# The Mixer's tenth load buffer, the order of sums in the first FFN sets, and the bank order of the up products

## The chip, the cores and the metric

The kernel runs on one core of a Trainium2 chip. The metric is device time in microseconds (us), the median of several runs; a profile is one execution taken by the hardware profiler. TensorE (PE in the profile) multiplies, VectorE (DVE) and ScalarE (ACT) work elementwise, GpSimd (POOL) and SyncE (SP) mostly issue transfers here. PEld is TensorE's weight load.

## The reference

One block of a network on 512 tokens of width 1024, in float32:

```python
x = x + 0.5 * swiglu(rmsnorm(x, g1), ffn1_w_gu, ffn1_w_down)      # D_FF = 2816
x = x + hybrid_mixer(rmsnorm(x, gm), w_in, ...)                   # convolution + gated linear attention
x = x + 0.5 * swiglu(rmsnorm(x, g2), ffn2_w_gu, ffn2_w_down)
out = rmsnorm(x, final_g)

def swiglu(x, w_gu, w_down):
    g, u = split(x @ w_gu, 2)
    return (silu(g) * u) @ w_down
```

`hybrid_mixer` multiplies x by `w_in` into conv inputs, q, k, v, a low-rank gate (`g_lr`, 16 columns), r and two output gates, and ends in `w_out_conv`, `w_out_gla` and `w_o`.

## The kernel before

**Products.** Each float32 product is made of three TensorE products of a high and a low part: `W.take()` gives a weight tile as `wh` (a ScalarE cast, L427) and `wl` (the rest, a VectorE subtraction, L430). Large products are done in *sets* by Strassen's scheme with seven products, named m1, p2, q6, p5, q7, p4, p3, each on sums of blocks of the weight and of the operand. The remaining columns are *plain units*: in each FFN one group of two up pairs (`mm_group`, four weight units of two k blocks each, over the eight k blocks of the width), and in the Mixer eight units for q and k (a group for heads 0 and 1 in four units, then four single columns) and eight of `w_out_conv`.

**The planner.** `PLAN` lists the weight blocks in order and `STEPS` the steps that use them, one unit or one of the seven products each. `Weights.issue` does one step: it starts loads ahead of time (`fetch`, `load_set`), makes sums of weight blocks (on VectorE at L404, or by an accumulating transfer on POOL at L390), and casts. It runs two steps ahead of the products. `Weights.slot(until)` picks the buffer for a load or sum: there are nine buffers of their own (`f0` to `f8`), and in the Mixer a tenth, which is a tile of the pool `op`. Each carries in `until` the last step that uses it; the one with the least value is taken. The tenth begins at -1. The pool `op` has 15 tiles and holds above all the high and low parts of the operands.

**The order of work.** The Tile framework plans each engine's queue when the program is built, from its own estimates of durations, mostly in the order in which the program is written among what it takes to be ready. `tc.issue_after(i)` holds the instructions of a block that run on the engine of `i` behind `i` in that engine's queue. `W.after_row`, `W.behind` and `W.lead` hand such an instruction to the next weight sum, the next cast and the next `wl`.

**Between FFN1 and the Mixer.** FFN1's down product ends in p4. Inside it, blocks of the result are transposed back (`back(i)`: L1281 on TensorE, L1285 on VectorE) and added to x, and `nxt.add(i)` makes the Mixer's operand for k block i (L541 on ScalarE, L542 on VectorE, squares at L552 and L553). The sum of p4's own result is L1222. `turned_out` and `turned_in` (L1183, L1189) turn other blocks by way of memory, on SyncE's queue; `grown` (L1272) adds them to x. The Mixer begins with `gl_raw`, a small load on SyncE (L1431) of the gate's 16 columns, which VectorE spreads into `gl_w` (L1437 to L1441). Its first group of products (L504) has `gate_k(k)` behind each k block: the transposes of block 4 + k for the first four, then two products of the gate (L1459, L1460) into an `aux` bank.

**An FFN's up sets.** The group gives the sums of two plain pairs in four banks; `plain_pair` multiplies the gate sums by the row of the norm (L1097) and applies Silu, and the result is multiplied into `hid[0]` later. Then ten sets run, each over two columns of g and u, in the order m1, p2, p5, q6, (next m1), q7, (next p2), p4, p3 for the first. `PairSet` keeps three pairs of PSUM banks for a set: a in `x`, b and c rotating over `w`, `z`, `y`; set 0 has b in `w` and c in `y`. `onto` adds a bank pair to a tile (two additions on L823), `whole` copies one half out (ScalarE, L830) and adds the other (VectorE, L831), `taken` makes the value of q6 or q7 (L813 to L815). p3 accumulates in c, so it can't start before the sum with c on q7 has been read. `banks("pairs", tags)` lays out the four tags in the order of the letters, two banks each.

**An FFN's down sets.** Two sets of 10 and 12 k blocks; `bank_of(new)` gives a set its banks: a the pair `A`, b two from `new`, c two more of the pool `mm`. The pool `mm` has six banks and `aux` two.

Of the kernel before, what the change touches and what calls it, by code (L numbers as in the profile page):

```python
# [11 lines left out]
AF = mybir.ActivationFunctionType  # L12
ALU = mybir.AluOpType
# [117 lines left out]
SLOTS = 9  # L131
# [62 lines left out]
def block_kernel(ctx: ExitStack, tc: tile.TileContext, xT, vecs, gf, gup, wgl, wts, out):  # L194
# [104 lines left out]
    class Weights:  # L299
# [3 lines left out]
        def __init__(self, ahead):  # L303
            self.ahead = ahead
            self.issued = 0
            self.taken = 0
            self.end = 0
            self.ready = []
            self.raw = {}
            self.loads = {}  # L310
            self.more = {}
            self.sums = {}
            self.first = {}
            self.until = [-1] * (SLOTS + 1)
            self.slots = SLOTS
            self.behind = None
            self.after_row = None
            self.lead = None
            self.added = None

# [30 lines left out]

        def slot(self, until):

            i = min(range(self.slots), key=lambda j: self.until[j])
            self.until[i] = until
            if i == SLOTS:
                return tile_of("op", [P, 1024])
            cnt[0] += 1
            return pools["f"].tile([P, 1024], F32, tag=f"f{i}", name=f"f{cnt[0]}")
# [33 lines left out]
        def issue(self):  # L393
            at = self.issued
            self.fetch(at)
            for n in self.loads.get(at, ()):
                self.load_set(n)
            for n in self.sums.get(at, ()):
                a11, _, a21, a22, _ = self.raw[n]
                w = unit_cols(PLAN[n])  # L400
                if not lean(n):
                    s3 = self.raw[n][4] = self.slot(STEPS.index((n, "q7")))
                    with ExitStack() if self.after_row is None else tc.issue_after(self.after_row):
                        self.summed = nc.vector.tensor_tensor(out=s3, in0=a11, in1=a21,  # L404
                                                              op=ALU.add).ins
                    self.after_row = None
                self.first[n] = (self.add(a21[:, :w], self.block(n + 3), self.added) if lean(n)
                                 else self.add(a21, a22))
            for n, i in self.more.get(at, ()):
                a = STEPS.index((n, ("p3", "p4")[i // 2]))  # L410
                self.raw[n][i] = self.dma(n + i, a)
            n, p = STEPS[at]
            w = unit_cols(PLAN[n])
            if p is None:
                raw = self.raw[n]
            else:
                a11, a12, a21, a22, s3 = self.raw[n]
                raw = {"m1": a11, "p2": a12, "q6": a11, "p5": a21, "q7": s3, "p4": a22,
                       "p3": a12}[p]
            if p == "q7" and lean(n):  # L420
                nc.vector.tensor_tensor(out=s3[:, :w], in0=a11[:, :w], in1=a22[:, :w],
                                        op=ALU.subtract)
            late = at >= len(STEPS) - len(pieces(HALVES[-1]))
            h = tile_of("op" if late else "wh", [P, 1024], F32R)
            l = tile_of("op" if late else "wl", [P, 1024], F32R)
            with ExitStack() if self.behind is None else tc.issue_after(self.behind):
                self.cast = nc.scalar.copy(h[:, :w], raw[:, :w]).ins  # L427
            self.behind = None
            with ExitStack() if self.lead is None else tc.issue_after(self.lead):
                nc.vector.tensor_tensor(out=l[:, :w], in0=raw[:, :w],  # L430
                                        in1=h[:, :w].bitcast(F32), op=ALU.subtract)
            self.lead = None
            if p == "m1":
                twin = n + 4 if STEPS[at + 1] == (n + 4, "m1") else n
                self.add(a11[:, :w], a21[:, :w], self.first[twin])
            if p == "p2":
                begins = STEPS[at - 1 : at + 2] == [(n, "m1"), (n, "p2"), (n, "p5")]
                self.add(a12[:, :w], a11[:, :w],
                         self.first[n + 4] if begins and not lean(n) else None)
            self.issued += 1  # L440
            self.ready.append((h, l))
# [316 lines left out]
    class PairSet:  # L758
# [58 lines left out]
        def onto(self, n, t):  # L817

            if not self.merged:
                nc.vector.tensor_tensor(out=t, in0=self.flat(n), in1=t, op=ALU.add)  # L820
                return
            for part in (self.left(n), self.right(n)):
                nc.vector.tensor_tensor(out=pair(t), in0=part, in1=pair(t), op=ALU.add)  # L823

        def whole(self, n):

# [218 lines left out]
    def ffn(up, down, norm, nxt, plain, at):  # L1045
# [5 lines left out]
        def finish(k):  # L1051
            if 3 <= k < 7:
                for i in (2 * k - 6, 2 * k - 5):
                    j = i // 4
                    nc.scalar.activation(
                        xn_tile[:, 2 * j : 2 * j + 2, i % 4], pair(x[i]), AF.Copy,
                        scale=vec[:, norm.goff + i : norm.goff + i + 1])
            if k == 0 and nxt is not None:
                square_ones()
            if k == at:  # L1060
                rows.append(norm.finish())
                W.after_row = norm.token
            if k == 6:
                xo.make("p5")

# [32 lines left out]
            nc.scalar.activation(s, s, AF.Silu)  # L1098
            gates.append(s)

        gates = []
        new_hid()
        for f in range(2):
            nc.scalar.copy(hid[-1][:, f], o[2 * f + 1])
# [12 lines left out]
        def up_set(i):  # L1117
            h = new_hid()

            def done(s, p):  # L1120
                if (i, p) in ((0, "m1"), (0, "q6")):
                    W.behind = s.group.taken
                if (i, p) == (0, "p2"):
                    xo.sum("q7")
                if (i, p) == (0, "q7"):
                    with tc.issue_after(xo.get("q7").last):
                        for f, t in enumerate(gates):
                            mul(hid[0][:, f], t, hid[0][:, f])
                if p == "p2":
                    if s.forked:  # L1130
                        g = s.whole("a")
                        s.g1 = g if s.merged else T()
                    else:
                        s.g1 = g = s.m1
                        s.onto("a", g)
                    s.g = g
                if p == ("p2" if i == last else "q7" if i == 0 else "q6"):
                    mul(pair(s.g1), pair(s.g), rows_of(0))
                    with tc.issue_after(W.cast) if i == 0 else ExitStack():
                        nc.scalar.activation(s.g1, s.g1, AF.Silu)  # L1140
                if (i, p) == (1, "p3"):
                    with tc.issue_after(s.group.taken):
                        norm.columns()
                if nxt is None and (i, p) in turns_in:
                    k = turns_in.index((i, p))
                    turned_in(XS[-1][:, k], turn[k])
                if nxt is None and (i, p) in turns_out:
                    turn.append(turned_out(XS[-1][:, len(turn)]))
                if p == ("p5" if i == last else "q7"):
                    s.onto("c", s.q7)  # L1150
                if p == "p4":
                    t = s.whole("b")
                    nc.vector.scalar_tensor_tensor(
                        out=h[:, :, :HW], in0=pair(t), scalar=-1.0, in1=pair(s.g1),
                        op0=ALU.mult, op1=ALU.mult)
                if p == "p3":
                    s.onto("c", s.q6)
                    mul(pair(s.q6), pair(s.q6), rows_of(1))
                    nc.scalar.activation(s.q6, s.q6, AF.Silu)
                    nc.vector.scalar_tensor_tensor(  # L1160
                        out=h[:, :, HW:], in0=pair(s.q7), scalar=-1.0, in1=pair(s.q6),
                        op0=ALU.mult, op1=ALU.mult)
                if p == "p3" and i == HALVES[0] - plain // 2:
                    downs.append(down_operands(0))
                    downs[0].early()

            return PairSet(xo, done, i, i != last)

        banks("pairs", "wxzy" if nxt is not None else "wzxy")
        run_sets(up_set)  # L1170
        banks()

# [20 lines left out]
    def down_product(downs, nxt, cols_of):  # L1193
# [52 lines left out]
        def bank_of(b):  # L1246
            return {"a": A, "b": [b() for _ in range(2)], "c": [MM(), MM()]}

        natural_set(downs[0], bank_of(AUX), first_done, HALVES[0])
        bank = bank_of(MM)  # L1250

        def done(p, o):
            c, l, scale = PLACE[p]
# [728 lines left out]
```

## Time and profile before

| | |
|---|---|
| median of 3 runs | 1155.37 us (1155.25 to 1156.33) |
| profiled execution | 1153.99 us, of which the span of the profile is 1152.3 us |
| mean granted clock of TensorE | 0.994 |
| VectorE busy | 1020.5 us (89%) |
| ScalarE busy | 724.3 us (63%) |
| POOL busy | 140.7 us (12%) |
| memory read and written | 133.46 MB and 11.53 MB, 126 GB/s over the span |

How to read the lines that follow: a group line has the line of the program, the engine, the operation, `out<-in` with buffer numbers left out, and the count. In a time line the first number is the start in us from the span's beginning, the second the time of the merged instructions, and the bracket gives the idle time of that engine before and what ended it. A line of waits reads: who waited, for whom, us in total, times, longest. A line of windows has the stretch, its length, the busy time of PE, PEld, DVE, ACT and POOL with counts, the granted clock (1.00 is full), the busy share of the DMA engines, and GB/s. SPq is SyncE's queue.

### The profile page before, as it was taken

How to read it: one execution, taken by the hardware profiler on the slowest of the kernel's cores; microseconds unless marked ns; L12 is line 12 of the kernel's file. 1: busy time of each engine (PE TensorE's matmuls, PEld its weight loads, DVE VectorE, ACT ScalarE, POOL GpSimd, SP SyncE). 2: the span in 40 equal slices, each digit the busy share in tenths (PEclk: the TensorE clock that was granted, in tenths of full speed). 3: DMA queues.
4: the chain of work that ended last, by engine and by line, in shares of the span. 5: the costliest groups of instructions: out<-in, count | busy, mean ns of one | idle time of the engine just before them, and what ended most of it. 6: DMA issues, size and time to landing. Idle time of an engine off the chain costs nothing.

```text
span 1152.3 us, 17536 instructions
## 1 busy us (share of the span) xinstructions
PE 1131.1 (98%) x6606; PEld 1000.9 (87%) x6606; DVE 1020.5 (89%) x1281; ACT 724.3 (63%) x997; POOL 140.7 (12%) x184
## 2 busy tenths in 40 slices
PE   9999999999969999999999999999999999999997
PEld 7788888988858889999999998899888888898885
DVE  8998889989776996979799989689989998989987
ACT  8666666676434755757485577555876666576635
POOL 1111111211111011110101100010011111111100
PEclk9999999999989999999999999999999999999999
DMA  8887777759575477876968867576467898877961
GB/s 295 179 216 166 195 194 196 200 131 279 140 244 146 110 180 186 231 190 158 231 177 235 208 177 223 124 181 171 115 152 191 229 228 223 200 209 175 249 142 73
DMA packets 75268, 217.45 MB, mean 189 GB/s; under 512 B 8272, under 2 KB 20688, under 8 KB 75184
## 3 DMA queue, kind: packets, MB, share of 16 engines
q0 software_dynamic: 22240, 79.18, 37.7%
q1 hardware_dynamic: 48304, 132.67, 33.7%
q10 hardware_dynamic: 4640, 4.49, 1.2%
q8 instruction: 52, 0.85, 0.3%
q14 instruction: 32, 0.26, 0.1%
HBM read 133.46 MB, written 11.53 MB: 126 GB/s over the span
## 4 chain that ended last, share of the span: by engine, by line
PE 87%; DVE 5%; DMA 4%; issue 3%; ACT 1%; POOL 0%; SPq 0%; POOLq 0%; DVEq 0%; ACTq 0%
PE mm L624 15%; PE bb L636 12%; PE mm L997 11%; PE y L636 8%; PE z L636 8%; PE w L636 8%; PE mm L489 6%; PE mm L504 5%; PE aux L997 4%; PE x L636 4%; DVE wl L430 2%; DMA f<-f 1%; PE aux L624 1%; PE w L624 1%; DMA op<-wts 1%
## 5 line engine op out<-in xcount | busy, mean ns | idle before, releaser
L427 ACT CAST wh<-f 128x1024 fp32r<-128x1024 f32 (+1 forms) x359 | 365.9, 1031 | 235.4 <-PE mm L997 36.9
L430 DVE TENSOR_TENSOR wl<-f,wh 128x1024 fp32r<-128x1024 f32 (+1 forms) x359 | 425.1, 1193 | 48.4 <-ACT wh L427 48.2
L390 POOL DMA_DIRECT2D f<-f x132 | 113.9, 863 | 822.9 <-DVE wl L430 518.4
L997 PE MATMUL mm<-wh,op 128*128 128x512 f32 x544 | 135.1, 389 | 0.0
L624 PE MATMUL mm<-op,wh 128*128 128x256 f32 x960 | 125.8, 284 | 0.0
L997 PEld LDWEIGHTS mm<-wh,op 128*128 128x128 f32 x544 | 102.0, 188 | 21.1
L624 PEld LDWEIGHTS mm<-op,wh 128*128 128x128 f32 x960 | 119.8, 192 | 0.4
L636 PE MATMUL bb<-op,wh 128*128 128x512 f32 x384 | 97.1, 395 | 0.0
L636 PEld LDWEIGHTS bb<-op,wh 128*128 128x128 f32 x384 | 69.2, 189 | 12.5
L997 PE MATMUL mm<-wl,op 128*128 128x512 f32 x272 | 73.3, 389 | 0.0
L636 PE MATMUL y<-op,wh 128*128 128x512 f32 x264 | 66.5, 392 | 2.6 <-DVE tp L823 2.6
L624 PE MATMUL mm<-op,wl 128*128 128x256 f32 x480 | 67.5, 283 | 0.0
L636 PE MATMUL z<-op,wh 128*128 128x512 f32 x264 | 66.6, 391 | 0.0
L636 PE MATMUL w<-op,wh 128*128 128x512 f32 x264 | 66.3, 391 | 0.2 <-DVE op L935 0.2
L624 PEld LDWEIGHTS mm<-op,wl 128*128 128x128 f32 x480 | 61.9, 192 | 0.1
L997 PEld LDWEIGHTS mm<-wl,op 128*128 128x128 f32 x272 | 51.0, 188 | 10.8 <-DVE wl L430 0.2
L636 PEld LDWEIGHTS y<-op,wh 128*128 128x128 f32 x264 | 48.1, 188 | 12.5 <-DVE tp L823 3.5
L504 PE MATMUL mm<-op,wh 128*128 128x512 f32 x192 | 49.8, 403 | 9.0 <-ACT wh L427 9.0
L636 PEld LDWEIGHTS w<-op,wh 128*128 128x128 f32 x264 | 48.2, 188 | 9.5 <-issue 0.4
L636 PEld LDWEIGHTS z<-op,wh 128*128 128x128 f32 x264 | 48.1, 188 | 8.9
L636 PEld LDWEIGHTS bb<-op,wl 128*128 128x128 f32 x384 | 52.4, 190 | 3.8
L636 PE MATMUL bb<-op,wl 128*128 128x256 f32 x384 | 53.5, 282 | 0.0
(368 smaller groups left out, 2018.6 us busy)
## 6 DMA issues: line engine op xcount, KB each, us to landing
f<-wts SPq DMA_DIRECT2D x207, 512.0 KB, 5.1
f<-f POOLq DMA_DIRECT2D x128, 512.0 KB, 5.4
f<-wts POOLq DMA_DIRECT2D x10, 512.0 KB, 8.8
op<-wts SPq DMA_DIRECT2D x8, 512.0 KB, 6.4
turn<-tp SPq DMA_DIRECT2D x12, 256.0 KB, 4.2
f<-wts SPq DMA_DIRECT2D x10, 256.0 KB, 4.6
X<-xT SPq DMA_DIRECT2D x8, 256.0 KB, 5.4
xs<-X POOLq DMA_DIRECT2D x8, 256.0 KB, 6.6
```

What stands on the lines that cost most here:

```text
L390: self.added = nc.gpsimd.dma_start(out_, a, accum_op=ALU.add).ins
L427: self.cast = nc.scalar.copy(h[:, :w], raw[:, :w]).ins
L430: nc.vector.tensor_tensor(out=l[:, :w], in0=raw[:, :w], in1=h[:, :w].bitcast(F32), op=ALU.subtract)
L489: nc.tensor.matmul(o, w[:, i * P : (i + 1) * P], a[k], start=j == k == 0, stop=j == 2 and k == kt - 1)
L504: nc.tensor.matmul(o_, w[:, s : s + P], a[k], start=k == 0 and j == 0, stop=k == kt - 1 and j == 2)
L624: nc.tensor.matmul(o[:, e * HW : (e + 1) * HW], w[:, k * HW + e * P : k * HW + (e + 1) * P], a(k), start=self.fresh and j == k == e == 0, ...
L636: nc.tensor.matmul(o[:, e, :n], w[:, k * HW + e * P : k * HW + (e + 1) * P], a(k), start=self.fresh and i == k == 0, stop=i == 1 and k == ...
L997: nc.tensor.matmul(o[t], a(k)[:, t * P : (t + 1) * P], ww[:, i * 512 : (i + 1) * 512], start=fresh and j == k == 0, stop=j == 2 and k == s ...
```

## The change

Three edits, in seven places:

1. `slot` chooses among ten buffers only while the step being issued is one of a set (`STEPS[self.issued][1] is not None`); while it is a plain unit it chooses among nine. This bears on the Mixer alone, since elsewhere there are nine.
2. In the first set of each FFN, the sum of q7 with bank c comes straight behind q7's value; behind it, by `issue_after`, stand the gate's product with the row, the next weight sum (`W.sum_after`, the new name of `after_row`), the second set's `whole("a")` and the next `wl` (`W.lead`). The plain pairs' two products move from q7 to p3, behind the sum with c there. The Silu of set 0 stays behind a cast.
3. The up banks lie in the order w, x, y, z in both FFNs (before: w, x, z, y and w, z, x, y), and the first down set takes its b banks from `mm`, the second from `aux` (before the other way round).

```diff
         def slot(self, until):
-            i = min(range(self.slots), key=lambda j: self.until[j])
+            n = self.slots if STEPS[self.issued][1] is not None else SLOTS
+            i = min(range(n), key=lambda j: self.until[j])
...
             for part in (self.left(n), self.right(n)):
-                nc.vector.tensor_tensor(out=pair(t), in0=part, in1=pair(t), op=ALU.add)
+                at = nc.vector.tensor_tensor(out=pair(t), in0=part, in1=pair(t), op=ALU.add)
+            return at.ins
...
-                if (i, p) == (0, "q7"):
-                    with tc.issue_after(xo.get("q7").last):
-                        for f, t in enumerate(gates):
-                            mul(hid[0][:, f], t, hid[0][:, f])
                 if p == "p2":
                     if s.forked:
-                        g = s.whole("a")
+                        with tc.issue_after(first_onto[0]):
+                            g = s.whole("a")
+                        if i == 1:
+                            W.lead = first_onto[0]
...
-                if p == ("p2" if i == last else "q7" if i == 0 else "q6"):
+                if p == ("p5" if i == last else "q7"):
+                    summed = s.onto("c", s.q7)
+                if (i, p) == (0, "q7"):
+                    first_onto.append(summed)
+                    W.sum_after = summed
+                    with tc.issue_after(summed), tc.issue_after(W.cast):
+                        mul(pair(s.g1), pair(s.g), rows_of(0))
+                        nc.scalar.activation(s.g1, s.g1, AF.Silu)
+                elif p == ("p2" if i == last else "q6") and i > 0:
                     mul(pair(s.g1), pair(s.g), rows_of(0))
-                    with tc.issue_after(W.cast) if i == 0 else ExitStack():
-                        nc.scalar.activation(s.g1, s.g1, AF.Silu)
+                    nc.scalar.activation(s.g1, s.g1, AF.Silu)
...
-                if p == ("p5" if i == last else "q7"):
-                    s.onto("c", s.q7)
...
                 if p == "p3":
-                    s.onto("c", s.q6)
+                    summed = s.onto("c", s.q6)
+                    if i == 0:
+                        with tc.issue_after(summed):
+                            for f, t in enumerate(gates):
+                                mul(hid[0][:, f], t, hid[0][:, f])
...
-        banks("pairs", "wxzy" if nxt is not None else "wzxy")
+        banks("pairs", "wxyz")
...
-        natural_set(downs[0], bank_of(AUX), first_done, HALVES[0])
-        bank = bank_of(MM)
+        natural_set(downs[0], bank_of(MM), first_done, HALVES[0])
+        bank = bank_of(AUX)
```

More of the change, by code (lines that the diff above doesn't have):

```diff
@@ L316, in __init__ @@
             self.behind = None
-            self.after_row = None
+            self.sum_after = None
             self.lead = None
@@ L402, in issue @@
                     s3 = self.raw[n][4] = self.slot(STEPS.index((n, "q7")))
-                    with ExitStack() if self.after_row is None else tc.issue_after(self.after_row):
+                    with ExitStack() if self.sum_after is None else tc.issue_after(self.sum_after):
                         self.summed = nc.vector.tensor_tensor(out=s3, in0=a11, in1=a21,
                                                               op=ALU.add).ins
-                    self.after_row = None
+                    self.sum_after = None
                 self.first[n] = (self.add(a21[:, :w], self.block(n + 3), self.added) if lean(n)
@@ L1061, in finish @@
                 rows.append(norm.finish())
-                W.after_row = norm.token
+                W.sum_after = norm.token
             if k == 6:
@@ L1099, in plain_pair @@
             gates.append(s)
-        gates = []
+        gates, first_onto = [], []
         new_hid()
```

## The prediction

> **What bounds the kernel now.** I read the page's head first, then the waits of TensorE, then the time line of each engine around the two longest of those waits, then the clock by windows.
>
> ```profile
> span 1152.3 us, 17536 instructions
> PE 1131.1 (98%) x6606; PEld 1000.9 (87%) x6606; DVE 1020.5 (89%) x1281; ACT 724.3 (63%) x997; POOL 140.7 (12%) x184
> ```
> ```profile
> PE mm L504 <- ACT wh L427: 9.0, 2, 8.7
> PE y L636 <- DVE tp L823: 2.6, 2, 2.1
> ```
>
> TensorE works for 98% of the span, and no part of the change adds or removes a matmul. Time can only come from its 1152.3 - 1131.1 = 21.2 us of idleness and from stretches at a low clock, or be lost in new ones. The edits touch the two rows above: 8.7 us, where the Mixer's first weight unit begins, and the waits on L823 in the first set of each FFN, 2.1 and 0.5 us. The rest of the idleness lies mostly behind the last product, which the change leaves alone. Where TensorE never idles, a microsecond saved early arrives at the end whole. First the large wait, on TensorE's time line:
>
> ```profile
> 331.46 1.08 PE L997 MATMUL mm<-wl,op 128*128 128x512 f32 x4
> 341.25 3.78 PE L504 MATMUL mm<-op,wh 128*128 128x512 f32 x8 [8.71 <-ACT wh L427]
> ...
> 346.14 0.38 PE L1281 MATMUL mm<-ident,op 128*128 128x128 f32 x2
> 346.27 0.47 PE L1459 MATMUL aux<-op,g 128*96 128x512 f32 x1
> ...
> 346.82 1.98 PE L504 MATMUL mm<-op,wh 128*128 128x512 f32 x8
> ...
> 349.55 0.38 PE L1281 MATMUL mm<-ident,op 128*128 128x128 f32 x2
> ```
>
> FFN1's last product ends at 331.46 + 1.08 = 332.54, the Mixer's first begins 8.71 us later. The twelve products of its first k take 346.14 - 341.25 = 4.89 us, the same twelve of the next k 349.55 - 346.82 = 2.73 us. So the stop costs 8.71 + (4.89 - 2.73 = 2.16) = 10.9 us. The second part is the clock (the column PEclk):
>
> ```profile
> 332.50:335.40 2.90, 0.04 (x1) 0.00 (x0) 2.90 (x5) 1.76 (x4) 0.90 (x2) 1.00 0.93 308
> 335.40:341.20 5.80, 0.00 (x0) 0.00 (x0) 2.15 (x4) 1.05 (x2) 1.27 (x2) 0.50 0.94 361
> 341.20:345.60 4.40, 4.36 (x10) 3.47 (x11) 4.39 (x11) 2.41 (x3) 0.00 (x0) 0.50 0.00 0
> ```
>
> The granted clock fell to 0.50 some 2.9 us after TensorE stopped and came back 4.4 us after it resumed. Why the unit was late stands in ScalarE's and SyncE's queues:
>
> ```profile
> 329.61 0.72 ACT L541 ACTIVATE op<-X,vec 128x512 fp32r<-128x512 f32 x1 [5.98 <-DVE X L1285]
> 340.15 1.04 ACT L427 CAST wh<-op 128x1024 fp32r<-128x1024 f32 x1 [5.89 <-DMA op<-wts]
> ```
> ```profile
> 254.69 53.90 SPq L364 DMA_DIRECT2D f<-wts  x14
> ...
> 313.93 0.33 SPq L364 DMA_DIRECT2D f<-wts  x1
> ...
> 320.03 8.08 SPq L1189 DMA_DIRECT2D tp<-turn  x15
> 328.21 1.79 SPq L364 DMA_DIRECT2D f<-wts  x4
> 330.12 0.52 SPq L364 DMA_DIRECT2D op<-wts  x1
> 336.26 0.33 SPq L1431 DMA_DIRECT2D tp<-wgl  x1
> ```
> `slot` gives a load the buffer whose `until` is least. The tenth has -1 at the Mixer's start, so unit 0 gets it: an `op` tile, one of 15 that FFN1's operands still hold. Units 1 to 3 got `f` buffers that FFN1's sums for q7 had left, and were issued early (the last two of the row of 14, and 313.93). Unit 0, needed first, was issued last, behind 15 small loads and four weight loads, and its cast could begin 340.15 - 330.12 = 10.0 us later.
>
> **The change, part by part.** *Tenth buffer in block sets only.* While the issued step is a plain unit, `slot` chooses among nine. Each of the eight first units moves up one buffer: unit 0 takes what unit 1 had and is issued before 254.69 + 53.90 = 308.6. Its cast needs one of three `wh` buffers; one comes free with each product step of about 2.7 us, so it falls into ScalarE's 5.98 us of idleness before 329.61. Its `wl` follows on VectorE, which waits there for L1285. The operand of k 0 is cast by 329.61 + 0.72 = 330.33, so the products can begin at 332.54 with nothing between. No load is added; unit 5 moves into the group at 328.21, and one V load takes the place of the `op` load behind it, so the DMA engines stay as full (0.94 above). V's own loads now wait for units 0 to 4 instead of FFN1's last steps and units 0 to 3, one unit later; a unit takes two k, 5.5 us, and V begins after unit 7, so at least three units (16 us) cover a load of 10 us. It costs nothing; without that cover each late load would cost the rest of its 10 us.
>
> What is late next is the gate weight. TensorE's order has L1281 and L1459 after each k, and these need rows that do not move with the load:
>
> ```profile
> 336.15 1.40 DVE L1222 SCALAR_TENSOR_TENSOR op<-mm,cols,tp 128x512 f32<-128x512 f32 x2
> 341.21 0.30 DVE L1437 CAST g<-tp 128x64 fp32r<-128x64 f32 x2 [3.66 <-DMA tp<-wgl]
> 341.72 0.63 DVE L1441 CAST g<-g 128x128 fp32r<-128x128 f32 x4
> ```
>
> The transposes L1281 need L1222, done at 337.55; the gate products L1459 need L1441, done at 342.35, since the small load `tp<-wgl` leaves SyncE only at 336.26 and lands 4.9 us later. Before, TensorE reached L1459 at 346.27, so both were hidden. Now the first k ends at 332.54 + 2.73 = 335.27, the second at 338.0, the third at 341.1 with a pair of transposes (0.38). What the gain is depends on how many k the planner puts ahead of the first gate product: all that fill the time to 342.35 give the whole 10.9 us; one gives 346.27 - 342.35 = 3.9 us less a second fall of the clock (2.2), 1.7 us. The planner does put work past a late operand: in the first set it issued three products of `z` before the waiting `y` (below). But it must believe that the operand is late; in the old order it put L1459 straight behind the first k, so its belief lies before the truth. I take the middle, L1459 in the third k near 339.7, an idle time of 342.35 - 339.7 = 2.7 us, too short for the clock to fall by the windows above: 10.9 - 2.7 = 8.2 us. Bounds: 1.7 and 10.9.
>
> The clock bears on this choice. [...]
>
> *First FFN sets.* VectorE's and TensorE's rows at the first set:
>
> ```profile
> 48.54 0.68 DVE L610 TENSOR_TENSOR tp<-tp,row 128x512 f32<-128x512 f32 x1
> ...
> 50.88 1.22 DVE L404 TENSOR_TENSOR f<-f,f 128x1024 f32<-128x1024 f32 x1
> 52.02 0.68 DVE L823 TENSOR_TENSOR tp<-y,tp 128x512 f32<-128x512 f32 x1
> 52.62 0.68 DVE L831 TENSOR_TENSOR tp<-x,tp 128x512 f32<-128x512 f32 x1
> 53.21 0.68 DVE L823 TENSOR_TENSOR tp<-y,tp 128x512 f32<-128x512 f32 x1
> ```
> ```profile
> 50.97 0.87 PE L636 MATMUL z<-op,wh 128*128 128x512 f32 x3
> 53.94 2.11 PE L636 MATMUL y<-op,wh 128*128 128x512 f32 x8 [2.10 <-DVE tp L823]
> ```
>
> Bank `y` is read by both L823 until 53.89, and p3 wants it from 50.97. Five instructions leave the way ahead of that: the plain pairs' two products (same shape as the L610 shown, 0.68 each), the gate's L610 (0.68), L404 (1.22) and L831 (0.68), together 3.9 us, so L823 ends near 50.0 and the 2.10 us go. FFN2 takes the same order: 0.5. Sum 2.6 us, with 0 as the lower bound, if ScalarE's copies come late instead. The moved work is hidden behind later sets, and the plain products' tiles, held until then, make at most eight of the nine `tp` buffers: the plain products' results are needed only by the down product, and L404's follower on POOL starts no later, since L404 now begins near 50.0 against 50.88. The `wl` held behind L823 (`lead`) is two steps ahead of its use. If VectorE, which has no gap here, fell one `wl` behind, TensorE would pay one `wl`, 1.2 us.
>
> *Bank order and the down sets.* "wxyz" puts `y` on banks that the plain pairs' sums occupy, and p5 opens it 33.76 - 30.85 = 2.9 us after the last is read:
>
> ```profile
> 29.57 1.28 DVE L1097 TENSOR_TENSOR tp<-mm,row 128x512 f32<-128x512 f32 x2
> 33.76 2.00 PE L636 MATMUL y<-op,wh 128*128 128x512 f32 x8
> ```
>
> So it costs nothing; without that cover it would cost one L1097, 0.6 us. The first down set now takes `mm` banks that `x` and `z` left sets earlier, the second `aux`; its p4 is read by L1222 until 337.55, before the gate products that want `aux` can start. TensorE has no wait of over 0.3 us at either place now, so there is no gain to be had: 0, at worst 0.6 us.
>
> **Sum.** 8.2 + 2.6 = 10.8 us. The profiled execution took 1153.99 us (span 1152.3), the median of the runs is 1155.37, 1.4 above; I take the gain off the median: 1144.6.
>
> **Rivals.**
> 1. *The whole stop goes*: four k stand ahead of the gate products, or the small load lands sooner. 10.9 + 2.6 = 13.5 us: 1141.9. For it: unit 1 holds two more k of ready work; against it the old order of L1459. 0.27.
> 2. *The gate weight takes the load's place and the clock falls again*: one or two k ahead, an idle time over 2.9 us. Two k: TensorE waits from 338.4 to 342.35, 4.0 us, and the clock adds 2.2, so 4.7 us remain; one k leaves 1.7. With 2.6: 1148.1 to 1151.1. 0.23. [...]
> 3. *Unit 0 stays late*, since its cast finds no `wh` or ScalarE's order keeps it behind L541 and L552: only the FFN part, 1152.8. ScalarE's idle row speaks against it. 0.04.
> 4. *Slower: a sum enters the tenth buffer ahead of the output sets.* With the new rotation the L404 of the second output set writes the `op` tile in place of a load. A load for an `op` tile waited there, harmlessly, on SyncE:
>
> ```profile
> SPq L364 <- PE mm L489: 19.8, 1, 19.8
> ```
>
> On VectorE the same wait would hold all `wl` behind it. Two product steps of lead (2 x 2.7 us) cover it in part; 19.8 - 5.4 = 14.4 us lost against 10.8 gained: 1159.0. It decides from 16.2 us of waiting on. Against it: that sum is issued only when the first output set is under way, behind the last L489. 0.04.
>
> **How the numbers follow.** The forecast (0.38) spans idle times of 1.2 to 2.9 us with 1.4 to 2.6 us from the FFN sets: gains of 8.0 + 1.4 to 9.7 + 2.6 us, 1143.1 to 1146.0. Gains that later waits eat up, within 0.2% (2.3 us, about what a measurement can tell from no change): 0.04. Faster: 0.38 + 0.27 + 0.23 + 0.04 = 0.92; same 0.04; slower 0.04. The range 1140.8 to 1150.8 leaves out rivals 3 and 4, the last case and the tail of rival 2.
>
> **What would show it.** Right: ScalarE casts unit 0 from an `f` tile near 325; L504 follows L997 without idleness; the next wait of TensorE is on L1441 or L1222, under 3 us, and PEclk stays at 1.00 there; `y` at L636 no longer waits on L823. Wrong: PEclk 0.50 after 336, an idle row ahead of L1459 of 4 us or more, L404 writing `op` with a long wait near 740, or a new wait of TensorE on a `wl` in the first sets.

## The result, and the profile after

The changed kernel took 1142.62 us (median of 4 runs, 1142.17 to 1142.89) against 1155.31 us of the kernel before on the same chip (4 runs, 1154.42 to 1156.33): ratio 0.9889, 95% interval 0.9872 to 0.9907. Its profiled execution took 1142.56 us. Up to line 353 the lines of the two kernels agree; behind it they are shifted, mostly by 1 to 10 (L430 is now L431, L504 is L505, L636 is L637, L823 is L824, L1459 is L1469).

The page's head and all of TensorE's waits on the sets' weights, after:

```profile
span 1140.8 us, 17541 instructions
PE 1130.0 (99%) x6606; PEld 1000.7 (88%) x6606; DVE 1019.4 (89%) x1281; ACT 724.3 (63%) x997; POOL 139.7 (12%) x184
```
```profile
PE z L637 <- DVE wl L431: 1.2, 1, 1.2
...
PE y L637 <- DVE wl L431: 0.2, 1, 0.2
```

The span of the profiled execution fell by 11.5 us; by the medians 12.7 us came off, since the execution profiled before (1153.99 us) was one of the faster ones of its kernel. The 8.7 us on L427 are gone from the waits, and so are the 2.6 us on L823; the two rows on `wl` are new. First the Mixer's start: the time lines of TensorE, ScalarE and VectorE, and the windows (columns as before).

```profile
330.99 1.08 PE L999 MATMUL aux<-wl,op 128*128 128x512 f32 x4
331.91 1.98 PE L505 MATMUL mm<-op,wh 128*128 128x512 f32 x8
...
342.63 0.39 PE L505 MATMUL mm<-op,wl 128*128 128x512 f32 x1
342.94 0.47 PE L1469 MATMUL aux<-op,g 128*96 128x512 f32 x1
```
```profile
324.84 1.06 ACT L428 CAST wh<-f 128x1024 fp32r<-128x1024 f32 x1 [1.67 <-DVE tp L1232]
```
```profile
341.39 0.30 DVE L1447 CAST g<-tp 128x64 fp32r<-128x64 f32 x2 [0.28 <-DMA tp<-wgl]
...
342.53 0.63 DVE L1451 CAST g<-g 128x128 fp32r<-128x128 f32 x4
```
```profile
332.00:342.30 10.30, 10.30 (x50) 8.43 (x49) 10.02 (x18) 7.26 (x12) 3.18 (x7) 1.00 1.01 344
```

Unit 0 is cast from an `f` tile at 324.84, L505 follows L999 with no idleness, and in the 10.3 us in which TensorE had mostly stood still it is busy for 10.30 at full clock. The last cast of the gate weight ends no sooner than before (343.16 against 342.35), but the planner put nearly four k ahead of the first gate product, which begins at 342.94, when the first two of these four casts are done, without TensorE standing idle. The whole stop of 10.9 us went.

In the first FFN set the time lines of TensorE, VectorE and ScalarE are these:

```profile
50.56 2.00 PE L637 MATMUL y<-op,wh 128*128 128x512 f32 x8
...
75.18 1.22 PE L637 MATMUL y<-op,wl 128*128 128x256 f32 x8 [0.25 <-DVE wl L431]
77.60 1.19 PE L637 MATMUL z<-op,wl 128*128 128x256 f32 x8 [1.21 <-DVE wl L431]
```
```profile
48.90 1.42 DVE L824 TENSOR_TENSOR tp<-y,tp 128x512 f32<-128x512 f32 x2
...
58.37 1.28 DVE L611 TENSOR_TENSOR hidw<-tp,hidw 128x512 f32<-128x512 f32 x2
...
61.97 2.36 DVE L431 TENSOR_TENSOR wl<-f,wh 128x1024 fp32r<-128x1024 f32 x2
```
```profile
71.73 1.05 ACT L428 CAST wh<-f 128x1024 fp32r<-128x1024 f32 x1 [4.63 <-DMA f<-f]
```

L824 ends at 50.3, so `y` starts at 50.56 without the 2.10 us. But some 25 us later TensorE waits for two `wl`, because ScalarE's cast at 71.73 had waited 4.63 us for an accumulating transfer (`f<-f`, issued by POOL). That transfer waits for the `wl` at 61.97, which now has the plain pairs' two products (58.37) ahead of it. How the transfer fared before and after, by the DMA issues in a window around it (the last number is us from issue to landing):

```profile
63.16 0.86 POOL L390 DMA_DIRECT2D f<-f  x1 [8.46 <-DVE wl L430]
```
```profile
f<-f POOLq DMA_DIRECT2D x1, 512.0 KB, 5.4
```
```profile
63.73 0.86 POOL L391 DMA_DIRECT2D f<-f  x1 [9.92 <-DVE wl L431]
```
```profile
f<-f POOLq DMA_DIRECT2D x1, 512.0 KB, 7.9
```

The first two rows are of before, the others of after: it left 0.57 us later and took 2.5 us longer, while TensorE was 2.8 us ahead (its x product began at 70.13 before, at 67.32 after).

### The profile page after: what moved, and what is told of

It reads as the page before. It is cut to its first block, busy times and chain, and to the rows that moved or that the text cites. A ratio compares the mean times of both kernels' runs of the same rounds, so it can differ in the third digit from the quotient of the medians.

```text
span 1140.8 us, 17541 instructions
## 1 busy us (share of the span) xinstructions
PE 1130.0 (99%) x6606; PEld 1000.7 (88%) x6606; DVE 1019.4 (89%) x1281; ACT 724.3 (63%) x997; POOL 139.7 (12%) x184
## 4 chain that ended last, share of the span: by engine, by line
PE 85%; DVE 7%; DMA 3%; issue 3%; ACT 1%; POOL 0%; POOLq 0%; DVEq 0%; ACTq 0%
PE mm L625 15%; PE mm L999 13%; PE bb L637 12%; PE w L637 7%; PE z L637 7%; PE y L637 7%; PE mm L490 6%; PE mm L505 5%; PE x L637 4%; PE aux L999 3%; DMA f<-f 3%; DVE wl L431 2%; PE aux L625 1%; PE w L625 1%; PE y L625 1%
## 5 line engine op out<-in xcount | busy, mean ns | idle before, releaser
L431 DVE TENSOR_TENSOR wl<-f,wh 128x1024 fp32r<-128x1024 f32 (+1 forms) x358 | 425.4, 1197 | 42.6 <-ACT wh L428 42.2
L391 POOL DMA_DIRECT2D f<-f x124 | 107.0, 865 | 756.5 <-DVE wl L431 459.1
L999 PE MATMUL mm<-wh,op 128*128 128x512 f32 x536 | 133.7, 389 | 0.0
L999 PEld LDWEIGHTS mm<-wh,op 128*128 128x128 f32 x536 | 100.4, 188 | 20.8
L637 PE MATMUL bb<-op,wh 128*128 128x512 f32 x384 | 97.1, 395 | 0.0
L637 PEld LDWEIGHTS bb<-op,wh 128*128 128x128 f32 x384 | 69.2, 189 | 12.5
L999 PE MATMUL mm<-wl,op 128*128 128x512 f32 x268 | 72.8, 389 | 0.0
L637 PE MATMUL y<-op,wh 128*128 128x512 f32 x264 | 66.5, 392 | 0.1
L637 PE MATMUL w<-op,wh 128*128 128x512 f32 x264 | 66.2, 391 | 0.0
L637 PE MATMUL z<-op,wh 128*128 128x512 f32 x264 | 66.2, 391 | 0.0
L999 PEld LDWEIGHTS mm<-wl,op 128*128 128x128 f32 x268 | 50.2, 188 | 10.6 <-DVE wl L431 0.2
L637 PEld LDWEIGHTS y<-op,wh 128*128 128x128 f32 x264 | 48.0, 188 | 9.4 <-ACT tp L815 0.5
L637 PEld LDWEIGHTS z<-op,wh 128*128 128x128 f32 x264 | 48.2, 188 | 9.1
L637 PEld LDWEIGHTS w<-op,wh 128*128 128x128 f32 x264 | 48.2, 188 | 9.1
L637 PEld LDWEIGHTS bb<-op,wl 128*128 128x128 f32 x384 | 52.4, 190 | 3.8
L637 PE MATMUL bb<-op,wl 128*128 128x256 f32 x384 | 53.5, 282 | 0.0
L846 DVE TENSOR_TENSOR op<-hidw,op 128x1024 fp32r<-128x1024 f32 (+2 forms) x56 | 49.1, 892 | 0.0
```

Source lines behind the costliest of these rows:

```text
L391: self.added = nc.gpsimd.dma_start(out_, a, accum_op=ALU.add).ins
L431: nc.vector.tensor_tensor(out=l[:, :w], in0=raw[:, :w], in1=h[:, :w].bitcast(F32), op=ALU.subtract)
L637: nc.tensor.matmul(o[:, e, :n], w[:, k * HW + e * P : k * HW + (e + 1) * P], a(k), start=self.fresh and i == k == 0, stop=i == 1 and k == ...
L846: nc.vector.tensor_tensor(out=l, in0=a, in1=h.bitcast(F32), op=ALU.subtract)
L999: nc.tensor.matmul(o[t], a(k)[:, t * P : (t + 1) * P], ww[:, i * 512 : (i + 1) * 512], start=fresh and j == k == 0, stop=j == 2 and k == s ...
```

## The experiments

Two theories stood after this. Of the Mixer: unit 0's buffer alone made the stop, so the edit of `slot` is nearly the whole gain. Of the sets: the two products that were moved made a transfer late and slow, and so gave the gain back. The rivals: the bank order carries part of the gain; VectorE is full, so the order within it is of no account; the late transfer was chance. Ratios are against the kernel before on the same chip.

**The change in three.** Each edit alone on the kernel before. e1 takes `slot`:

```diff
-            i = min(range(self.slots), key=lambda j: self.until[j])
+            n = self.slots if STEPS[self.issued][1] is not None else SLOTS
+            i = min(range(n), key=lambda j: self.until[j])
```

> The kernel before with the edit of slot alone. Theory (the stop at the Mixer's start is nearly the whole gain, and it came from unit 0 holding the tenth buffer): 10.9 us less than before, 8.71 of idleness and 2.16 of half clock, so about 1144.4 us, ratio 0.9906; ScalarE casts unit 0 from an f tile near 325 and the first L504 follows L997 without idleness; the row y <- tp L823 of 2.1 us stays. Rival (the prediction's sum: 8.2 us from the stop and 2.6 from the sets): 1147.1 us, ratio 0.9929. Rival (the stop goes only together with the new bank order of the down sets, since their a, b and c banks decide when the Mixer's group gets its own): under 3 us, ratio over 0.997.

1144.52 us, ratio 0.9895 (0.9882 to 0.9909), span 1140.9. The stop is gone whole, and the set's wait stays:

```profile
PE y L637 <- DVE tp L824: 2.6, 2, 2.1
```

This one edit has the time of the whole change within the intervals. Its profiled execution took 1142.6 us at a mean granted clock of 0.999, its other three 1144.38 to 1145.53 us at 0.997. Behind the same wait of 2.1 us the clock was at 0.50 for 3.41 us in e3's trace, below; that it fell in these three is not shown, since there is no trace of them.

e2 takes the order in the first sets, without `slot` and banks:

```diff
+                if (i, p) == (0, "q7"):
+                    first_onto.append(summed)
+                    W.sum_after = summed
...
+                    if i == 0:
+                        with tc.issue_after(summed):
+                            for f, t in enumerate(gates):
+                                mul(hid[0][:, f], t, hid[0][:, f])
```

> The kernel before with the new order of the first FFN sets alone; slot and banks are the old ones. The prediction: 2.6 us less, 1152.7 us, ratio 0.9978. Theory (the 2.1 us return 25 us later as a wait of p5's and p4's wl, because VectorE has no gap there and the plain pairs' two products, put behind p3, push the wl that the accumulating transfer waits for): 0.3 to 0.8 us less, ratio 0.9993 to 0.9998, with TensorE waiting on L431 for 1.2 to 1.5 us between 74 and 79. Rival (the late wait in the changed kernel was chance, one slow transfer of 7.9 us instead of 5.4): no wait on L431 there and 2 us or more less. The stop of 8.7 us ahead of the Mixer stays in any case.

1155.72 us, ratio 0.9997 (0.9988 to 1.0006): no gain is measured. TensorE's waits on `wl` in its sets:

```profile
PE z L636 <- DVE wl L430: 1.2, 1, 1.2
...
PE w L636 <- DVE wl L430: 0.7, 1, 0.7
```

The 1.2 us are at 77.19, as in the changed kernel, and the transfer took 7.7 us, so it was no chance. The 0.7 us lie in FFN2, in place of its 0.5. The time of e2 is not that of the sets alone: in its trace ScalarE's first L541 for the Mixer began at 328.74 instead of 329.61, but the Mixer's stop was 10.36 us, against 8.71 before and 9.89 in e3, which has the same code there. The stop is thus not the same in every trace.

e3 takes the banks:

```diff
-        banks("pairs", "wxzy" if nxt is not None else "wzxy")
+        banks("pairs", "wxyz")
...
-        natural_set(downs[0], bank_of(AUX), first_done, HALVES[0])
-        bank = bank_of(MM)
+        natural_set(downs[0], bank_of(MM), first_done, HALVES[0])
+        bank = bank_of(AUX)
```

> The kernel before with the new bank order alone: w, x, y, z in both FFNs, and the two down sets with their b banks exchanged. The prediction and the theory: 0, at worst 0.6 us more, ratio 1.0000 to 1.0005, no new wait of TensorE over 0.3 us. Rival (the bank order carries part of the gain: the down sets' banks come free earlier, so that the four k ahead of the gate products become possible, or the group starts earlier): 1 us or more less, ratio under 0.999.

1156.27 us, ratio 1.0001 (0.9992 to 1.001). The rival of the banks falls. The trace shows one thing more, on TensorE's time line:

```profile
53.98 3.63 PE L636 MATMUL y<-op,wh 128*128 128x512 f32 x8 [2.10 <-DVE tp L823]
```

Behind the same wait of 2.10 us the eight products took 3.63 us instead of the 2.11 of the kernel before, since the clock was at 0.50 from 53.88 to 57.29. So the wait on L823 cost 1.5 us more than its length here. The trace before has the same wait with the clock at 1.00 behind it, and e1 has it at a mean clock of 0.999 over its span; what divides these from e3 is not shown (the last section has the rows of before and e3).

**What the tenth buffer costs.** e4 lets every unit but the first take it, so that unit 1 gets the `op` tile:

```diff
-            i = min(range(self.slots), key=lambda j: self.until[j])
+            n = SLOTS if self.issued == ENDS[0] and self.spared < 1 else self.slots
+            self.spared += self.issued == ENDS[0]
+            i = min(range(n), key=lambda j: self.until[j])
```

> The kernel before, but the Mixer's first load alone may not take the tenth buffer: unit 0 gets an f buffer and unit 1 the op tile. Theory (what costs is who holds the tenth buffer: the load into it leaves at 330 and lands near 340 whichever unit it is): ScalarE casts unit 1 from op near 340; TensorE does unit 0's two k at once (332.5 to 338) and then waits 3 to 4 us for unit 1, so of the 10.9 us some 7 come back, less another 2.2 if the clock falls again: 1146.5 to 1151, ratio 0.992 to 0.996. Rival (any unit in the tenth buffer costs the whole stop, since it binds the op tile that the operands want): under 2 us gained, ratio over 0.998. Rival (the tenth is harmless for any unit but the first): the whole 10.9 us, ratio 0.9905.

1150.0 us, ratio 0.9949 (0.993 to 0.9968), span 1146.5. TensorE's and ScalarE's time lines:

```profile
342.31 0.96 PE L507 MATMUL mm<-op,wh 128*128 128x512 f32 x3 [3.15 <-ACT wh L430]
```
```profile
341.21 1.04 ACT L430 CAST wh<-op 128x1024 fp32r<-128x1024 f32 x1
```

The load into the tenth buffer lands late whichever unit it is (issued at 330.42 it took 10.8 us here, issued at 330.12 it took 9.9 us before); TensorE does two k first and then waits 3.15 us instead of 8.71, with the clock at 0.50 from 344 to 346.6. The price is that of the unit's place in the order, as the theory has it.

e5 leaves unit 0 in the tenth buffer, and has POOL issue its load instead of SyncE:

```diff
-            nc.sync.dma_start(t[:, :w], self.block(n))
+            first = n == STEPS[ENDS[0]][0]
+            (nc.gpsimd if first else nc.sync).dma_start(t[:, :w], self.block(n))
```

> The kernel before with the load of the Mixer's unit 0 issued by POOL instead of SyncE; it still goes to the tenth buffer. Theory A (SyncE's queue is what made the load late: it stood behind 15 small loads of 8.1 us and four loads of weights, and the tile was free by then): the load leaves by 328 or earlier, lands by 336, and the stop of 8.71 us shrinks by 4 us or more; span 1146 to 1148. Theory B (the op tile is held by FFN1's operands until about 330): the load leaves at 329 to 331 on POOL too and the stop shrinks by less than 2 us; span 1150.5 to 1153.

1155.4 us, span 1153.7; the stop was 10.61 us. POOL's time line:

```profile
329.79 2.19 POOL L1391 DMA_DIRECT2D xs<-X  x4 [25.19 <-DVE X L1286]
331.97 0.54 POOL L365 DMA_DIRECT2D op<-wts  x1
```

The load left later than on SyncE (331.97 against 330.12), since the plan put it behind four copies of X that wait for L1286. So this does not tell whether the tile itself was free sooner; that stays open.

**The price of the gate weight.** e11 and e12 force on the changed kernel the orders that the prediction weighed: the fourth k, or the third, held behind the gate products of the k ahead.

```diff
-                        nc.tensor.matmul(o_, w[:, s : s + P], a[k], start=k == 0 and j == 0,
-                                         stop=k == kt - 1 and j == 2)
+                        with ExitStack() if late is None else tc.issue_after(late):
+                            nc.tensor.matmul(o_, w[:, s : s + P], a[k], start=k == 0 and j == 0,
+                                             stop=k == kt - 1 and j == 2)
                 if extra is not None:
-                    extra(k)
+                    late = extra(k)
...
-            nc.tensor.matmul(gps[:R3], w, xl[k], start=False, stop=k == KD - 1)
+            g = nc.tensor.matmul(gps[:R3], w, xl[k], start=False, stop=k == KD - 1)
+            return g.ins if k == 2 else None         # e12: k == 1
```

> The changed kernel, but the Mixer group's fourth k is held behind the gate products of the first three: the order that the prediction took for the likeliest. The prediction's price: TensorE reaches the gate products near 340.3 and waits 2.2 to 2.7 us for gl_w (done at 342.53 in the changed kernel, and it doesn't depend on TensorE's order); the clock does not fall within 2.9 us of idleness: 2.2 to 2.7 us more than the changed kernel, 1144.8 to 1145.3, ratio to before 0.9909 to 0.9915. Rival (later slack takes it back): under 0.5 us more. Rival (the clock falls at a shorter wait already): 4 us or more.

1143.88 us, ratio 0.9898 (0.9884 to 0.9912), 1.3 us over the changed kernel's median. TensorE's time line:

```profile
341.63 0.47 PE L1471 MATMUL aux<-op,g 128*96 128x512 f32 x1 [1.40 <-DVE g L1453]
```

The mechanism is as priced, the size is half: TensorE came to the gate products at 340.2, and the last cast of `gl_w` ended at 341.85, sooner than in the changed kernel (343.16).

> The same with the third k held behind the gate products of the first two, the prediction's second rival. TensorE reaches them near 337.4 and is idle until 342.9 but for some transposes, 4.6 to 5.2 us in one stretch or in two; if in one, the clock falls as before the change and adds 2.2 us: 1147.2 to 1150 us, ratio to before 0.993 to 0.9955. If the transposes split the wait into stretches under 2.9 us, the clock stays: 4.6 to 5.2 us more alone, 1147.2 to 1147.8.

1149.75 us, ratio 0.9952 (0.9936 to 0.9968). TensorE's time line, then the windows:

```profile
338.98 0.77 PE L1293 MATMUL mm<-ident,op 128*128 128x128 f32 x4 [1.03 <-DVE X L1297]
342.24 0.47 PE L1471 MATMUL aux<-op,g 128*96 128x512 f32 x1 [2.49 <-DVE g L1453]
...
343.53 3.28 PE L507 MATMUL mm<-op,wh 128*128 128x512 f32 x8
```
```profile
339.75:342.24 2.49, 0.00 (x1) 0.01 (x1) 2.19 (x10) 1.58 (x3) 0.57 (x2) 1.00 0.90 245
342.24:342.90 0.66, 0.66 (x3) 0.53 (x4) 0.66 (x3) 0.00 (x0) 0.00 (x0) 0.98 0.98 292
342.90:346.30 3.40, 3.40 (x10) 2.57 (x9) 2.91 (x7) 1.61 (x3) 1.07 (x2) 0.50 1.02 414
```

7.1 us over the changed kernel, in the forecast span, but by another way than either branch of the expectation: the wait was split (0.22, 1.03 and 2.49 us), none reached 2.9 us, and the clock fell to 0.50 all the same, 0.7 us after TensorE had resumed. The eight products that take 1.98 us elsewhere took 3.28.

**The first sets.** Three kernels move the plain pairs' two products in the changed kernel and leave all else. e9 puts them back where they were:

```diff
                     xo.sum("q7")
+                if (i, p) == (0, "q7"):
+                    with tc.issue_after(xo.get("q7").last):
+                        for f, t in enumerate(gates):
+                            mul(hid[0][:, f], t, hid[0][:, f])
...
-                    if i == 0:
-                        with tc.issue_after(summed):
-                            for f, t in enumerate(gates):
-                                mul(hid[0][:, f], t, hid[0][:, f])
```

> The changed kernel, but the plain pairs' two products stay where they were before, right behind the sum of operands for q7; the other parts of the new order stay. Theory (1.3 us of VectorE's work either ahead of the sum with c or ahead of the transfer's wl): L824 ends near 51.6, so y at 50.6 waits 1 us, and the transfer leaves near 62.4 again as before, so the waits at 75 to 79 go: net 0.5 to 1.2 us less than the changed kernel, 1141.4 to 1142.1, ratio 0.9880 to 0.9887. Rival (the late transfer comes from the weight sum L405 being held behind the sum with c, not from the products): the waits at 75 to 79 stay and the 1 us at 50.6 is added: 1143.5, ratio 0.9899.

1141.4 us, ratio 0.9872 (0.9854 to 0.9891), span 1139.9. `y` waits 0.8 us on L824, the waits at 75 and 77.6 are gone, and the transfer takes 5.3 us. The weight sum L405, held as in the changed kernel, is not the cause.

e6 moves them on instead, behind p3 of the second set (late1) or of the third (late2):

```diff
-                    if i == 0:
+                    if i == 1:         # late2: i == 2
                         with tc.issue_after(summed):
```

> The changed kernel, but the plain pairs' two products go behind the second set's p3 instead of the first's. Theory (in the changed kernel these two, 1.3 us at 58.4, push the wl that the accumulating transfer waits for to 62 to 63; it leaves at 63.7, 0.7 us ahead of a load, shares the DMA engines with it and takes 7.9 us instead of 5.4, and so TensorE waits for wl between 75 and 79): the transfer leaves near 62.4, lands by 68.5, and the waits on L431 at 75 and 77.6 go: 1.5 us less than the changed kernel, about 1141.1 us, ratio to before 0.9877. Rival (VectorE is full from 43 to 66 whatever the order, and a sum or wl behind it is late all the same): the same as the changed kernel, 1142.6, ratio 0.989. Rival (the products now delay the wl of p5 and p4 of the second set, 77 to 80): the wait only moves, 1142.6 or more.

> The same with the two products behind the third set's p3, past the waits at 75 to 80; their tiles are held some 17 us longer. Theory: as for the second set's p3 or better, 1.5 to 2 us less than the changed kernel, 1140.6 to 1141.1 us, ratio to before 0.9873 to 0.9877; no wait on L431 before 100. Rival (VectorE is full whatever the order): 1142.6, ratio 0.989. Rival (the two tiles held longer starve the sets of tp tiles): a new wait of ScalarE or VectorE for a tp tile, 1143 or more.

1139.85 us (1139.47 to 1140.51), ratio 0.986 (0.9844 to 0.9876), and 1140.15 us, ratio 0.9862 (0.9846 to 0.9877). These two are the fastest kernels of this study and are not told apart; late1 is 2.8 us under the changed kernel's median, with no run of either in the other's spread. TensorE waits nowhere in the up sets on `wl` or L824. The rows of late1: POOL's and VectorE's time lines, and the transfer's landing.

```profile
61.70 0.86 POOL L391 DMA_DIRECT2D f<-f  x1 [8.12 <-DVE wl L431]
```
```profile
59.95 1.22 DVE L431 TENSOR_TENSOR wl<-f,wh 128x1024 fp32r<-128x1024 f32 x1
...
75.67 1.28 DVE L611 TENSOR_TENSOR hidw<-tp,hidw 128x512 f32<-128x512 f32 x2
```
```profile
f<-f POOLq DMA_DIRECT2D x1, 512.0 KB, 5.3
```

With the products at 75.67, the `wl` comes at 59.95 instead of 61.97, and the transfer at 61.70 instead of 63.73. "VectorE is full, so the order is of no account" falls.

Why is the transfer slower when it is late? A load of SyncE stands behind it: issued 1.40 us after it before the change (64.56), 0.67 us after it in the changed kernel (64.40). The packets of POOL's queue (q0) and SyncE's (q1), before, in 2.9 us behind the load's issue, and after, in 4.5 us:

```profile
q0 software_dynamic: 122, 0.50, 110.0%
```
```profile
q0 software_dynamic: 135, 0.51, 68.9%
q1 hardware_dynamic: 120, 0.49, 28.9%
```

Before, all 122 packets of these 2.9 us are the transfer's: the load issued at 64.56 had none until past 67.4. After, both queues moved packets in the same 4.5 us (135 and 120), and the load issued at 64.40 had its first by 66.4. In twelve traces the load follows the transfer. In those with 1.28 to 1.62 us between the two the transfer took 5.1 to 5.4 us (before, e1, e3, e4, e5, e9, late1, late2), in those with 0.67 or 0.68 us it took 7.0 to 7.9 us (after, e2, e11, e12). These four also share the new order of VectorE, so the load itself has to be moved to tell. e10 takes the load out of the way in the changed kernel:

```diff
+            if n == 20:
+                self.held = t, n
+                return t
             nc.sync.dma_start(t[:, :w], self.block(n))
...
+                if n == 13:
+                    t, m = self.held
+                    with tc.issue_after(self.added):
+                        nc.gpsimd.dma_start(t, self.block(m))
```

> The changed kernel, but one load (a22 of the fourth set, the one that SyncE issues at 64.40, 0.67 us behind the accumulating transfer of 63.73) is issued by POOL behind that transfer. VectorE's order is that of the changed kernel, so the wl ahead of the transfer stays as late. Theory (the transfer takes 7.9 us instead of 5.4 because the load shares the DMA engines with it from its start): the transfer lands in 5.3 to 5.5 us, near 69.2, and the waits of TensorE on wl at 75 and 77.6 shrink from 1.46 us to under 0.5: 1.2 to 2.2 us less than the changed kernel's 1142.6, ratio to before 0.987 to 0.988. Rival (VectorE's delay of 0.6 us alone makes TensorE wait; the length of the transfer is hidden): waits and time as in the changed kernel, ratio 0.989. Rival (what makes it long is something else, such as its place in time): it takes 7.7 to 7.9 us again.

1144.64 us, ratio 0.9905 (0.9891 to 0.9919), span 1142.9. Issued at 63.88, as late as in the changed kernel, the transfer took 6.0 us, and the waits at 75 and 77.6 went: the length of the transfer, not the 0.57 us alone, made them. That it took 6.0 and not 5.3 us stays open. The time was missed by more than 3 us, since a new wait came at 95, and the clock fell to 0.50 behind it (row in the last section):

```profile
PE w L644 <- DVE wl L434: 2.2, 1, 2.2
```
```profile
95.33 1.60 PE L644 MATMUL w<-op,wl 128*128 128x256 f32 x8 [2.23 <-DVE wl L434]
96.73 3.21 PE L644 MATMUL w<-op,wh 128*128 128x512 f32 x8
```

The cast ahead of this `wl` waited for a transfer that POOL issued at 86.88. The load that was moved left at 71.03 and took 6.2 us, and the transfers behind it left at 77.77 and 86.88, where the changed kernel has 72.28 and 81.82. That the moved load made the wait is read from the order of these times and was not tested alone. The two rows took 1.7 us more than at full clock (1.11 and 2.00).

## Why the prediction was right or wrong

- *The tenth buffer, 8.2 us forecast.* The mechanism was right (unit 0 cast from `f` at 324.84, forecast near 325; no idleness; clock 1.00), the term was mis-sized: all 10.9 us of the execution profiled came back. The step that failed is "I take the middle, L1459 in the third k": the planner put nearly four k ahead, as rival 1 had it. With the order that was assumed the price is 1.3 us (e11), not 2.7, so 9.6 us would have been the right middle.
- *An idle time of 2.7 us, "too short for the clock to fall by the windows above".* Wrong by e10, where the clock fell to 0.50 with a wait of 2.23 us, and by e3, where it did with one of 2.10 us (last section). The 2.9 us of the windows was read from one fall in one execution and is not a bound for the wait. In the changed kernel nothing hung on this step, since TensorE did not wait there.
- *The first sets, 2.6 us forecast.* The step that failed is "the moved work is hidden behind later sets". The wait on L823 went as forecast, and the sign of failure that the text named, a new wait on a `wl`, came: 1.2 us at 77.6 and 0.2 at 75. The sum of it is 11.5 - 10.9 = 0.6 us by the spans of before and after, 0.1 by those of e1 and after (1140.9 and 1140.8), and nothing that e2 could measure. The clause on "one `wl` behind" had the mechanism and its 1.2 us; taken as the value and not as an aside, it would have left 1.4 us. What it lacked was the chain by way of the transfer. Put one set later the same two products leave 3.1 us by the spans of e1 and late1 (1140.9 and 1137.8), so the forecast size was there to be had. The term also lacked the fall of the clock to 0.50 that came with the wait on L823 in e3's trace, 1.5 us more there. By the medians of e1 and the changed kernel (1144.52 and 1142.62) the sets could be worth 1.9 us; their intervals overlap, so this stays open.
- *Banks, 0.* Right (e3: 1.0001).
- *The sum.* 10.8 us forecast, 11.5 by the spans: 2.7 us too little in one term and 2.0 too much in the other nearly cancelled, which is luck. The time, 1142.62, lies in the stated range but below the 1143.1 to 1146.0 that the forecast's own mechanism spanned. Of the 2.0 us between 1142.62 and 1144.6, some 1.2 come from reading the gain in one execution and taking it off the median: by the medians it was 12.7, not 11.5.
- *Rivals.* The first had the Mixer's start right, and 1141.9 only with 2.6 us from the sets that did not come. The second (gate weight and clock) is what e12 shows when it is forced: 1149.75, inside its 1148.1 to 1151.1, though that figure counted 2.6 us from the sets that are not there. The third left no row. Of the fourth the first half came true: L405 wrote an `op` tile at 724.92, but VectorE had waited only 0.89 us for L490 there, and TensorE did not wait.

## What to carry to other kernels

A buffer chosen by "least recently needed" can hand the most urgent load the buffer that is ready last: give the first items of a phase buffers that are surely free, and keep the risky one for items that are needed well after it comes free (with the second unit in it, e4, the kernel took 1150.0 us, against 1144.52 in e1). Work moved off a critical chain must be put behind every chain that the same engine feeds, not only behind the one in view: here 1.3 us of VectorE's work, moved 14 us on, fell on the `wl` that released a transfer, and one set later TensorE had no wait from it. Where an order is written by hand, measure each part alone: one of the three edits was nearly the whole gain. And count a wait of TensorE with the clock in mind: here waits of 2.1 to 2.5 us cost up to 1.7 us more than their length.

## What the runs showed of the hardware

- The clock was low behind some waits of TensorE and not behind others. In the trace before it was at 0.50 from 335.41 to 345.65, 10.24 us, with the wait of 8.71 us. With e3's wait of 2.10 us, which ended at 53.98, it was at 0.50 from 53.88 to 57.29; with e10's of 2.23 us, which ended at 95.33, from 95.92 to 99.34; with e12's of 1.03 and 2.49 us, the last of which ended at 342.24, from 342.90 to 346.30: 3.41, 3.42 and 3.40 us. With e4's of 3.15 us, which ended at 342.31, it was at 0.50 from 344 to 346.6 (0.59 in the 1 us ahead of that). It stayed at 1.00 with the wait of 2.10 us in the kernel before, which ended at 53.94, with 1.40 us in e11 and with 1.21 us in the changed kernel. The windows before, then of e3 and e10 (the second column is the length, the third TensorE's busy time, the third from the end the clock):

```profile
52.10:55.52 3.42, 1.58 (x7) 1.32 (x8) 3.42 (x5) 0.64 (x2) 0.86 (x1) 1.00 0.27 90
```
```profile
50.47:53.88 3.41, 1.40 (x9) 0.93 (x7) 3.41 (x6) 2.31 (x4) 0.86 (x1) 1.00 0.92 205
53.88:57.29 3.41, 3.31 (x8) 2.64 (x9) 3.41 (x5) 0.00 (x0) 0.00 (x0) 0.50 1.03 199
```
```profile
92.51:95.92 3.41, 1.18 (x10) 0.98 (x10) 1.87 (x3) 2.95 (x5) 0.85 (x1) 1.00 0.39 76
95.92:99.34 3.42, 3.42 (x13) 2.83 (x12) 3.42 (x5) 0.96 (x2) 0.86 (x1) 0.50 0.70 116
```

TensorE was idle for 1.84 of the 3.42 us of the row before, where the clock stayed, and for 2.01 and 2.23 of the 3.41 us that ended as the clock fell in e3 and e10. How much idleness the clock bears is not told by this: no run varied a wait alone.

- In the first FFN set the accumulating transfer of 512 KB took 5.1 to 5.4 us in the eight traces in which a load was issued 1.28 to 1.62 us behind it, 7.0 to 7.9 us in the four with 0.67 or 0.68 us, and 6.0 us in e10, where that load was moved.
- The gate weight's small load, issued sooner, did not land sooner: it left SyncE at 332.53 instead of 336.26 and took 8.8 us instead of 4.9, so it landed at 341.3 instead of 341.2. In the window quoted above (332.00 to 342.30) the busy share of the DMA engines was 1.01.
